# Rotary embedding on one core: loads issued eight tiles ahead, alternating with the stores in one software queue

## The chip, the cores and the metric

The kernel runs on one core of a Trainium2 chip. The time is that of the device for one execution, in microseconds (us); the median over several executions is compared. The kernel uses three parts of the core: VectorE (DVE in the profile) computes, GpSimd (POOL) issues every DMA, and the core's 16 DMA engines move the data between the chip's memory (HBM) and the on-chip SBUF.

## The reference

`x` has 8 batches, 2048 positions, 8 heads and 64 values per head, in float32: 33.55 MB. The output has the same shape and type. `cos` and `sin` have 2048 positions by 32 values.

```
x1, x2 = x[..., :32], x[..., 32:]
out1 = x1 * cos - x2 * sin
out2 = x1 * sin + x2 * cos
out  = concatenate([out1, out2], axis=-1)
```

Each input value is read once and each output value is written once; only the two small tables are used again.

## The kernel before

**Tiles.** The 2048 positions are laid over 128 partitions, 16 neighbouring positions to each. A tile is one batch and four of these 16 positions: 128 partitions by 4 x 512 = 2048 values. There are 8 x 4 = 32 tiles. In HBM a tile is 1 MB of float32, in 128 contiguous pieces of 8 KB; in SBUF it is 512 KB of bfloat16. The conversion in either direction is made by the DMA itself, so that a load reads 1 MB and writes 512 KB, and a store reads 512 KB and writes 1 MB.

**Loads and stores.** All DMAs are issued by POOL (`nc.gpsimd.dma_start`) and so go through one software queue, in the order in which the program writes them: first the two tables (L44, L45), then all 32 loads (L70) from a loop of their own, then the 32 stores (L101) from the loop that computes. POOL runs its instructions in this order. Before it issues one, it waits for what that DMA needs, and everything behind it waits too. The tile framework gives the DMAs of this queue eight completion semaphores in turn, so that a DMA also waits until the one eight places before it has landed: never more than eight are under way.

**Compute.** For each tile DVE runs four instructions: `t1 = x * cos` (L91) and `t2 = x * sin` (L92) over the whole tile, then a subtraction (L98) and an addition (L99) over half a tile each, which put the output tile `ot` together. The framework's scheduler orders them over neighbouring tiles: through much of the program L91 of the next tile stands before L98 of this one.

**Buffers.** 20 for the input tiles (`xpool`), 4 each for `t1` and `t2`, 12 for the output tiles (`opool`). Load 20 and later ones wait until DVE is done with the tile 20 places before. L98 of tile 12 and later ones waits until the store of the tile 12 places before has landed; as the first store stands behind the last load in the queue, DVE can run no further than 12 output tiles before that.

Of the kernel before, what the change touches and what calls it, by code (L numbers as in the profile page):

```python
# [2 lines left out]

# [4 lines left out]


@with_exitstack  # L10
def kernel(
    ctx: ExitStack,
    tc: tile.TileContext,
    x: bass.AP,
    cos: bass.AP,
    sin: bass.AP,
    out: bass.AP,
):
    nc = tc.nc
    f32 = mybir.dt.float32  # L20
    bf16 = mybir.dt.bfloat16

    B, S, H, D = x.shape
    Dh = D // 2
    P = 128
    HD = H * D
    R = S // P

    SL = 4
    n_blk = R // SL  # L30
    FREE = SL * HD
    NH = SL * H
    NK = NH * 2

    xv = x.rearrange("b (q r) h d -> b q r (h d)", q=P)
    ov = out.rearrange("b (q r) h d -> b q r (h d)", q=P)

    cos_src = cos.rearrange("(q r) d -> q r d", q=P)
    sin_src = sin.rearrange("(q r) d -> q r d", q=P)

    const_pool = ctx.enter_context(tc.tile_pool(name="const", bufs=1))
    cos_sb = const_pool.tile([P, R, Dh], bf16, tag="cb")
    sin_sb = const_pool.tile([P, R, Dh], bf16, tag="sb")
    nc.gpsimd.dma_start(out=cos_sb, in_=cos_src)  # L44
    nc.gpsimd.dma_start(out=sin_sb, in_=sin_src)  # L45

    num_tiles = B * n_blk

    xpool = ctx.enter_context(tc.tile_pool(name="xpool", bufs=20))
    tpool = ctx.enter_context(tc.tile_pool(name="tpool", bufs=4))  # L50
    opool = ctx.enter_context(tc.tile_pool(name="opool", bufs=12))

    def coef(tab, l):
        a = tab[:, l * SL, :]
        return dataclasses.replace(
            a, ap=[a.ap[0][:], [Dh, SL], [0, 2 * H], a.ap[1][:]]
        )

    def idx(t):
        b = t // n_blk  # L60
        l = t % n_blk
        return b, l

    eng = nc.vector

    xts = []
    for t in range(num_tiles):
        b, l = idx(t)
        xt = xpool.tile([P, FREE], bf16, tag="xt", name=f"xt{t}")
        nc.gpsimd.dma_start(  # L70
            out=xt.rearrange("p (r f) -> p r f", r=SL),
            in_=xv[b, :, l * SL : (l + 1) * SL, :],
        )
        xts.append(xt)

    for t in range(num_tiles):
        b, l = idx(t)
        xt = xts[t]

        t1 = tpool.tile([P, FREE], bf16, tag="t1")  # L80
        t2 = tpool.tile([P, FREE], bf16, tag="t2")
        ot = opool.tile([P, FREE], bf16, tag="ot")

        cb = coef(cos_sb, l)
        sb = coef(sin_sb, l)

        xtv = xt.rearrange("p (r k d) -> p r k d", r=SL, d=Dh)
        t1k = t1.rearrange("p (r k d) -> p r k d", r=SL, d=Dh)
        t2k = t2.rearrange("p (r k d) -> p r k d", r=SL, d=Dh)

        eng.tensor_mul(out=t1k, in0=xtv, in1=cb)  # L91
        eng.tensor_mul(out=t2k, in0=xtv, in1=sb)  # L92

        t1v = t1.rearrange("p (h d) -> p h d", d=D)
        t2v = t2.rearrange("p (h d) -> p h d", d=D)
        otv = ot.rearrange("p (h d) -> p h d", d=D)

        eng.tensor_sub(out=otv[:, :, 0:Dh], in0=t1v[:, :, 0:Dh], in1=t2v[:, :, Dh:D])  # L98
        eng.tensor_add(out=otv[:, :, Dh:D], in0=t2v[:, :, 0:Dh], in1=t1v[:, :, Dh:D])  # L99

        nc.gpsimd.dma_start(  # L101
            out=ov[b, :, l * SL : (l + 1) * SL, :],
            in_=ot.rearrange("p (r f) -> p r f", r=SL),
        )


# [1 line left out]
_INS = ['x', 'cos', 'sin']  # L108
_OUTS = [((8, 2048, 8, 64), 'float32')]


# [23 lines left out]
```

## Time and profile before

| | us |
|---|---|
| median of 5 runs | 169.62 |
| lowest and highest of the 5 | 168.74, 170.59 |
| the profiled execution's own time | 170.7 |
| its span (first to last instruction) | 168.9 |
| DVE busy, 128 instructions | 111.7 |
| POOL busy, 70 instructions | 35.3 |

The span is the part of the profiled execution that the trace covers; 1.8 us of its time lie around it. The page gives the busy time of each engine, then the span in 40 equal slices of 4.2 us with the busy share of the engines and the DMA engines and the data rate, then the DMA queue, the chain of work that ended last, and the groups of instructions with their waits. The rate in GB/s counts the bytes that a DMA writes at its destination: for a load that is bfloat16, half of what it reads. A DMA share above 1 means that the records of neighbouring packets on a DMA engine overlap a little. A POOL line with an idle time and "<-DMA xt" says that POOL waited until a load had landed.

### The profile page before, as it was taken

How to read it: one execution, taken by the hardware profiler on the slowest of the kernel's cores; microseconds unless marked ns; L12 is line 12 of the kernel's file. 1: busy time of each engine (PE TensorE's matmuls, PEld its weight loads, DVE VectorE, ACT ScalarE, POOL GpSimd, SP SyncE). 2: the span in 40 equal slices, each digit the busy share in tenths (PEclk: the TensorE clock that was granted, in tenths of full speed). 3: DMA queues.
4: the chain of work that ended last, by engine and by line, in shares of the span. 5: the costliest groups of instructions: out<-in, count | busy, mean ns of one | idle time of the engine just before them, and what ended most of it. 6: DMA issues, size and time to landing. Idle time of an engine off the chain costs nothing.

```text
span 168.9 us, 282 instructions
## 1 busy us (share of the span) xinstructions
DVE 111.7 (66%) x128; POOL 35.3 (21%) x70
## 2 busy tenths in 40 slices
DVE  0049999999999960000007999999999999960000
POOL 7512122212212221221122122122212112120000
DMA  4999999999999999999999999999999999999940
GB/s 54 175 207 216 210 212 214 216 210 212 216 214 210 213 215 213 211 213 214 254 416 423 431 431 431 423 425 433 429 427 425 429 431 427 429 427 427 431 188 2
DMA packets 9506, 50.61 MB, mean 300 GB/s; under 512 B 1056, under 2 KB 1312, under 8 KB 5408
## 3 DMA queue, kind: packets, MB, share of 16 engines
q0 software_dynamic: 9504, 50.60, 103.2%
q14 instruction: 2, 0.02, 0.0%
HBM read 34.08 MB, written 33.55 MB: 400 GB/s over the span
## 4 chain that ended last, share of the span: by engine, by line
DMA 51%; DVE 24%; issue 12%; POOL 2%; POOLq 0%; DVEq 0%; PEldq 0%
DMA xt<-in_x_dram 39%; DMA out_dram<-ot 12%; DVE t L91 8%; DVE t L92 6%; DVE ot L98 5%; DVE ot L99 5%; POOL out_dram L101 2%; POOL cos_sb L44 0%; POOLq L130 0%; POOL sin_sb L45 0%; POOLq L101 0%; DVEq L98 0%; PEldq L130 0%; POOLq L70 0%
## 5 line engine op out<-in xcount | busy, mean ns | idle before, releaser
L91 DVE TENSOR_TENSOR t<-xt,cos_sb 128x2048 bf16<-128x2048 bf16 x32 | 38.9, 1216 | 11.1 <-DMA xt<-in_x_dram 10.9
L98 DVE TENSOR_TENSOR ot<-t,t 128x1024 bf16<-128x1024 bf16 x32 | 21.8, 681 | 27.7 <-DMA out_dram<-ot 27.7
L92 DVE TENSOR_TENSOR t<-xt,sin_sb 128x2048 bf16<-128x2048 bf16 x32 | 38.9, 1215 | 0.0
L101 POOL DMA_DIRECT2D out_dram<-ot x32 | 17.0, 532 | 65.9 <-DMA out_dram<-ot 29.1
L70 POOL DMA_DIRECT2D xt<-in_x_dram x32 | 16.9, 541 | 49.1 <-DMA xt<-in_x_dram 47.2
L99 DVE TENSOR_TENSOR ot<-t,t 128x1024 bf16<-128x1024 bf16 x32 | 21.8, 682 | 0.0
L44 POOL DMA_DIRECT2D cos_sb<-in_cos_dram x1 | 0.7, 667 | 0.8 <-PEq L130 0.8
L45 POOL DMA_DIRECT2D sin_sb<-in_sin_dram x1 | 0.5, 540 | 0.0
L119 POOL MEMSET const-float32-0.0<- 128x1 f32 x1 | 0.1, 98 | 0.2 <-issue 0.2
L119 POOL MEMSET const-bfloat16-1.0<- 128x1 bf16 x1 | 0.1, 101 | 0.0
L119 POOL MEMSET const-float32-1.0<- 128x1 f32 x1 | 0.1, 98 | 0.0
L119 POOL MEMSET const-uint8-127<- 128x1 uint8 x1 | 0.1, 98 | 0.0
## 6 DMA issues: line engine op xcount, KB each, us to landing
out_dram<-ot POOLq DMA_DIRECT2D x32, 1024.0 KB, 19.1
xt<-in_x_dram POOLq DMA_DIRECT2D x32, 512.0 KB, 19.1
cos_sb<-in_cos_dram POOLq DMA_DIRECT2D x1, 128.0 KB, 3.0
sin_sb<-in_sin_dram POOLq DMA_DIRECT2D x1, 128.0 KB, 3.0
```

The costliest lines, as they stand in the source:

```text
L44: nc.gpsimd.dma_start(out=cos_sb, in_=cos_src)
L45: nc.gpsimd.dma_start(out=sin_sb, in_=sin_src)
L70: nc.gpsimd.dma_start(out=xt.rearrange("p (r f) -> p r f", r=SL), in_=xv[b, :, l * SL : (l + 1) * SL, :],)
L91: eng.tensor_mul(out=t1k, in0=xtv, in1=cb)
L92: eng.tensor_mul(out=t2k, in0=xtv, in1=sb)
L98: eng.tensor_sub(out=otv[:, :, 0:Dh], in0=t1v[:, :, 0:Dh], in1=t2v[:, :, Dh:D])
L99: eng.tensor_add(out=otv[:, :, Dh:D], in0=t2v[:, :, 0:Dh], in1=t1v[:, :, Dh:D])
L101: nc.gpsimd.dma_start(out=ov[b, :, l * SL : (l + 1) * SL, :], in_=ot.rearrange("p (r f) -> p r f", r=SL),)
L119: nc = _bacc.Bacc("TRN2", target_bir_lowering=False, num_devices=1)
```

## The change

The loads leave their own loop. Eight loads are issued ahead of the computing loop; then each turn t of that loop first issues load t + 8 and at its end, as before, store t. In POOL's program the order becomes: the tables, loads 0 to 8, store 0, load 9, store 1, load 10, and so on to store 22, load 31, and then stores 23 to 31. The number of DMAs, their shapes, the buffers and DVE's instructions are unchanged. In DVE's program the scheduler's order of the 128 instructions shifts a little: through the first 18 tiles L91 of the next tile stands before L98 of this one, and from tile 19 on the four instructions of a tile stand together. All lines after the edit stand seven lower: loads L72, stores L108, DVE L98, L99, L105, L106.

```diff
-    xts = []
-    for t in range(num_tiles):
+    AHEAD = 8
+    xts = {}
+
+    def load(t):
         b, l = idx(t)
         xt = xpool.tile([P, FREE], bf16, tag="xt", name=f"xt{t}")
         nc.gpsimd.dma_start(
             out=xt.rearrange("p (r f) -> p r f", r=SL),
             in_=xv[b, :, l * SL : (l + 1) * SL, :],
         )
-        xts.append(xt)
+        xts[t] = xt
+
+    for t in range(AHEAD):
+        load(t)
 
     for t in range(num_tiles):
         b, l = idx(t)
         xt = xts[t]
+        if t + AHEAD < num_tiles:
+            load(t + AHEAD)
```

## The prediction

> **What bounds the kernel now.** I read the page's rows of slices first, then stretches of the span with DMA share and rate, then the waits, then the timeline of POOL, and the chain last.
>
> ```profile
> DMA  4999999999999999999999999999999999999940
> GB/s 54 175 207 216 210 212 214 216 210 212 216 214 210 213 215 213 211 213 214 254 416 423 431 431 431 423 425 433 429 427 425 429 431 427 429 427 427 431 188 2
> ...
> HBM read 34.08 MB, written 33.55 MB: 400 GB/s over the span
> ```
>
> The DMA engines are full from the second slice to the 38th. The rate has two plateaus because it counts bytes at the destination: 213 in the loads, which is 426 read from HBM, and 427 in the stores. Per HBM byte both stages run alike, one after the other.
>
> ```profile
> core 0: us, DVE busy (x) POOL busy (x), PEclk, DMA share, GB/s
> ...
> 10.00:82.00 72.00, 50.96 (x56) 15.33 (x29) 1.00 1.06 213
> ...
> 88.00:150.00 62.00, 60.25 (x72) 12.08 (x23) 1.00 1.12 428
> 150.00:160.00 10.00, 0.52 (x1) 0.67 (x2) 1.00 1.12 426
> ```
>
> From 150 to 160 us DVE and POOL are done and the rate is unchanged: the queue still drains. So DVE never set the rate, although it is busy for 60 of the 62 us before.
>
> ```profile
> POOL xt L70 <- DMA xt<-in_x_dram: 47.2, 23, 4.4
> POOL out_dram L101 <- DMA out_dram<-ot: 29.1, 15, 2.3
> DVE ot L98 <- DMA out_dram<-ot: 27.7, 1, 27.7
> POOL out_dram L101 <- DVE ot L99: 21.7, 9, 2.9
> ```
>
> POOL mostly waits for a DMA eight places earlier to land. DVE's 27.7 us are its wait for a free output buffer. The nine waits on DVE come last in the program; they shorten the queue but, by the stretches above, don't empty it.
>
> ```profile
> 2.44 4.24 POOL L70 DMA_DIRECT2D xt<-in_x_dram  x8
> 10.94 1.23 DVE L91 TENSOR_TENSOR t<-xt,cos_sb 128x2048 bf16<-128x2048 bf16 x1 [10.94 <-DMA xt<-in_x_dram]
> 11.12 0.53 POOL L70 DMA_DIRECT2D xt<-in_x_dram  x1 [4.44 <-DMA xt<-in_x_dram]
> ...
> 87.30 0.53 POOL L101 DMA_DIRECT2D out_dram<-ot  x1 [1.88 <-DMA xt<-in_x_dram]
> ...
> 89.84 0.53 POOL L101 DMA_DIRECT2D out_dram<-ot  x1 [2.00 <-DMA out_dram<-ot]
> ...
> 146.13 0.53 POOL L101 DMA_DIRECT2D out_dram<-ot  x1 [2.94 <-DVE ot L99]
> ...
> 149.61 0.53 POOL L101 DMA_DIRECT2D out_dram<-ot  x1 [2.94 <-DVE ot L99]
> 150.81 0.53 POOL L101 DMA_DIRECT2D out_dram<-ot  x1 [0.67 <-DVE ot L99]
> ```
>
> The view of the output tensor adds how long its stores took from issue to landing:
>
> ```profile
> DMA to landing us min/median/max: 13.4/19.1/19.5
> ```
>
> An issue stands 0.28 us behind the landing that it waited for. Load 0 lands at 10.84 (first L91 at 10.94), load 31 at 87.30 - 0.28 = 87.02: (87.30 - 11.12)/31 = 2.457 us per load. The shortest landing, 13.4 us, fits store 30: 149.61 + 13.4 = 163.0, and store 31 one step later, at about 165.5. So a store takes (165.5 - 87.0)/32 = 2.45 us. DVE at its own pace needs 149.61 - 146.13 = 3.48 us per tile.
>
> **The sum of the span now:** 10.84 (first load down) + 31 x 2.457 + 32 x 2.45 + 3.4 (end of the program, 168.9 - 165.5) = 168.8 of 168.9.
>
> ```profile
> DMA 51%; DVE 24%; issue 12%; POOL 2%; POOLq 0%; DVEq 0%; PEldq 0%
> ```
>
> The chain has 24% on DVE. That is no gain to be had: it follows a store back to the DVE tile that released its issue, but that store then stood 13 us or more in a full queue.
>
> **The change, part by part.**
>
> *The same 66 DMAs.* None is removed, added or resized; POOL's 64 issues of about 0.54 us (35 us) stay. What moves is order: stores 0 to 22 go ahead of loads 9 to 31. Each load moved past k stores lands 2.45k later, each store as much earlier. Nothing of the sum changes unless a DMA engine runs empty or a DMA's 2.45 us change.
>
> *The added wait at the start.* POOL now holds load 9 behind store 0, and store 0 needs tile 0 computed. DVE starts at 10.94 and needs L91, L92, L91 of the next tile (in by 13.3), L98 and L99: end 15.7 as in the timeline before. Store 0 goes at 15.9, load 9 at 16.5 instead of 13.57. At 15.9 loads 0 to 2 have landed (10.84 + 2 x 2.457 = 15.75), so loads 3 to 8, six DMAs or 14.7 us of work, cover the 2.9 us. Cost 0; without cover it would be 2.9 us, once.
>
> *The wait in the steady state.* Behind each waiting store stand all later loads. A pair of load and store takes 4.91 us in the queue, a tile on DVE 3.48. Store t is ready at 15.7 + 3.48t. Its place in the queue (the DMA eight before it landed) opens at 23.4 for store 2 (ready 22.7), 28.3 for store 3 (26.2), 33.2 for store 4 (29.7): the margin grows, and the queue holds eight again from load 10 on. Cost 0; the cover is gone only if DVE needed over 4.91 us per tile, and then each tile would pay the excess.
>
> *Buffers.* Load t + 8 overwrites tile t - 12, L98 of tile t needs store t - 12, landed long before. DVE's 27.7 us wait disappears and turns into waits of about 4.91 - 3.48 = 1.4 us per tile for its load. Both lie beside a full queue: worth 0.
>
> *The end.* Load 31 is followed by stores 23 to 31. It lands at 10.84 + 8 x 2.457 + 23 x 4.91 = 143.4; DVE finishes its tile 3.5 us later, store 31 goes at about 147.2 (150.81 now). Stores 24 to 30, seven, are then under way, so it lands in its turn, nine stores after load 31: 165.5. Cost 0.
>
> *The switches of direction.* This is the one price that the trace hardly shows. Before, the queue switches once from loads to stores and never back. After, 24 times to stores and 23 times back: 46 more. The one switch: from 87.30 to 89.84 is 2.54 where 2.457 is usual, +0.08 us.
>
> ```profile
> 83.00:83.50 0.50, 0.00 (x0) 0.00 (x0) 1.00 1.02 213
> 83.50:84.00 0.50, 0.00 (x0) 0.00 (x0) 1.00 1.05 328
> 84.00:84.50 0.50, 0.00 (x0) 0.00 (x0) 1.00 1.23 442
> ```
>
> In these half microseconds, while the engines go over to stores, the share stays above 1 and the rate climbs without a dip: no engine stops. The 0.08 us then look like a later landing of stores, which a switch back returns. Bounds per switch: above, for the unseen way back, a transfer that finds the pipe empty, `cos_sb`, with 3.0 us from issue to landing less 0.6 us for its 128 KB at 213 GB/s, so 2.4 x 23 = 55 us, far off; below nothing, the next load's reads overlapping the store's writes. A load writes and a store reads half of what passes the wide side, so with both ways wholly apart a pair would take 12/16 of its time: -1.23 us x 23 = -28 us. I take 0, the value nearest to the share at the switch.
>
> Weighed here: the rows say 426 read and 427 written, each alone. The Trainium skill, "DMA: Bandwidth & Descriptors", section "Latency and other measured facts", gives copies from HBM to HBM 214 GB/s in each direction as the full rate, 428 together; by it a mix has no more than one direction alone, the 67.6 MB take 158 us either way, and the sum stays. It speaks against a gain. The same page, "Two DMAs through the same engine are not ordered", says that the read and write sides of an engine are separate queues and descriptors are pipelined, which allows the overlap; by it the sum could fall by up to the 28 us. No run here mixes the two yet.
>
> **Sum:** span 168.9 + 0 = 168.9. The profiled execution took 170.7, 1.1 above the median; with no change in the span the forecast is the median, 169.6 us.
>
> **Rivals.**
>
> *Each switch costs (slower).* Place: the DMA engines, at each of 46 switches. At the row's 0.083 us: 46 x 0.083 = 3.8, so 173.4. It decides from 1.7/46 = 0.037 us on, which is 1% of the time. At twice the row it is 177. For it: the one switch did come late, and the way back is unseen. Against: the share without a dip.
>
> *Reads run ahead of writes (faster).* If at each way back an engine has read one packet of the next load while the store's last writes go out: a load is 8 packets on each engine (128 pieces over 16), so 2.457/8 = 0.31 us x 23 = 7.1, so 162.5. At the whole overlap, 169.6 - 28 = 141, with 3.68 us per pair just above DVE's 3.48. For it: shares of 1.06 and 1.12 say that neighbouring packets overlap already, by a few hundredths. Against: load and store take the same 2.45 us, as if the wide side alone counted, whichever it is.
>
> *The queue runs dry behind a store that waits for DVE (slower).* Needs a tile over 4.91 us; each 0.1 us above that is 2.3 us over 23 pairs. Against: DVE keeps 3.48, and even its four mean durations laid end to end (1216, 1215, 681 and 682 ns) are 3.79. Under 3 in 100, held within the slower share.
>
> **How the numbers follow.** About 1%, 1.7 us, is what a measurement here can tell from no change. No change in the DMA's rate: 0.50, its own range 168 to 171.3. Switches cost, or the queue runs dry: 0.30, of which 0.10 above 177. Reads run ahead: 0.20, of which 0.07 below 157, twice the one packet and a little less. The range 157 to 177 leaves out 0.17. Faster 0.20, same 0.50, slower 0.30.
>
> **What would show it.** Right: the two plateaus become one of about 320 GB/s in the slices between 30 and 145 us (a load's 0.524 and a store's 1.049 MB written in 4.91 us), the DMA share stays above 1, POOL's waits alternate between loads and stores landing, DVE waits 1.4 us per tile, the last store is issued near 147 us. Dear switches: a plateau under 315, pairs of POOL issues over 5 us apart. Overlap: a plateau over 325. A dry queue: tenths under 9 in the DMA row and long POOL waits on L106. I am wrong if the pair differs from 4.91 us by over 0.07.

## The result: 0.4% slower, and the profile after

| | before | after |
|---|---|---|
| median, us | 170.06 (93 runs) | 170.77 (53 runs) |
| lowest and highest, us | 168.44, 171.10 | 169.48, 171.44 |
| span of the profiled execution, us | 168.9 | 169.2 |

The ratio after to before is 1.0041, 95% interval 1.0030 to 1.0052. That is inside the 1% that the prediction called no change, and 1.2 us from its 169.6. But with this many runs the interval leaves out 1: the change costs 0.71 us, where the prediction's sum says 0.

The two plateaus have become one, as foreseen. From the page of after, the DMA share and the rate in 40 slices:

```profile
DMA  4999999999999999999999999999999999999960
GB/s 53 169 200 212 216 214 266 305 307 322 334 333 325 319 308 310 311 332 334 331 323 301 311 313 331 334 329 323 307 312 309 326 330 360 432 430 422 422 248 2
```

Stretches of after (columns as before):

```profile
core 0: us, DVE busy (x) POOL busy (x), PEclk, DMA share, GB/s
...
10.00:28.00 18.00, 17.24 (x19) 3.73 (x7) 1.00 1.06 210
...
34.00:142.00 108.00, 87.02 (x99) 23.48 (x45) 1.00 1.09 320
...
148.00:160.00 12.00, 0.00 (x0) 0.13 (x1) 1.00 1.12 428
```

The mixed stage runs at 320 GB/s with a share of 1.09, between 1.06 of the loads and 1.12 of the stores. POOL's waits changed places:

```profile
POOL out_dram L108 <- DMA out_dram<-ot: 49.3, 22, 2.6
POOL xt L72 <- DMA xt<-in_x_dram: 38.0, 23, 4.2
DVE t L98 <- DMA xt<-in_x_dram: 32.4, 19, 10.7
POOL out_dram L108 <- DMA xt<-in_x_dram: 12.3, 6, 2.7
POOL out_dram L108 <- DVE ot L106: 12.0, 4, 4.4
```

DVE's single wait of 27.7 us for an output buffer is gone. In its place stand waits for a load: 19, of which the first, 10.7 us, is the one at the start that before has too, and the other 18 make 21.7 us; POOL waits for DVE four times only. POOL's timeline in after:

```profile
15.84 0.54 POOL L108 DMA_DIRECT2D out_dram<-ot  x1 [4.42 <-DVE ot L106]
16.37 0.54 POOL L72 DMA_DIRECT2D xt<-in_x_dram  x1
...
31.01 0.53 POOL L72 DMA_DIRECT2D xt<-in_x_dram  x1 [1.66 <-DMA xt<-in_x_dram]
...
124.25 0.53 POOL L72 DMA_DIRECT2D xt<-in_x_dram  x1 [1.58 <-DMA xt<-in_x_dram]
...
147.60 0.53 POOL L108 DMA_DIRECT2D out_dram<-ot  x1 [2.95 <-DVE ot L106]
```

Store 0 and load 9 go at 15.84 and 16.37 (foreseen 15.9 and 16.5), the last store at 147.60 (147.2). From load 12 at 31.01 to load 31 at 124.25 lie 19 pairs: 4.907 us each, against 2.457 + 2.45 = 4.907 before. The chain names DVE no more:

```profile
DMA 81%; issue 3%; POOL 3%; POOLq 0%; PEldq 0%
```

Where, then, are the 0.71 us? The stretches of one microsecond around the first store, of before and of after:

```profile
25.00:26.00 1.00, 1.00 (x2) 0.10 (x1) 1.00 1.00 201
26.00:27.00 1.00, 1.00 (x2) 0.43 (x1) 1.00 1.14 229
27.00:28.00 1.00, 1.00 (x2) 0.00 (x0) 1.00 1.07 213
```

```profile
25.00:26.00 1.00, 1.00 (x3) 0.37 (x1) 1.00 1.21 229
26.00:27.00 1.00, 1.00 (x1) 0.16 (x1) 1.00 1.04 152
27.00:28.00 1.00, 1.00 (x2) 0.00 (x0) 1.00 0.94 209
```

In after the rate falls to 152 GB/s between 26 and 27 us, while the share of that microsecond is 1.04: the engines are not idle, their packets take longer. By the trace's packet records a packet of a load takes 0.324 us in the even stream; between 24 and 28 us 37 of them take over 0.4 in after, the longest 0.91, and none in before. The first packet of a store begins at 27.51, so the slow ones run ahead of it. They belong, but for those of the engines that lag, to load 8, the last load ahead of the first store. The trace also keeps, for each DMA, the moment at which each of the 16 engines reported its part. I call the mean of these 16, less that of the DMA before, the step of a DMA. It is 2.455 us on average in the even stream of both kernels; that of load 8 is 2.93 in after, 0.47 late, and 2.456 in before. Nothing later in after stands out so. The start differs as well, ahead of anything that the change moves: load 1 lands, on the mean, at 10.63 in before and 10.92 in after, and over the other profiles with this start (g2 aside) between 10.2 and 11.7. The slowest engine, which ends the program, runs behind the mean by 2.6 us at the end of before and by 2.1 at the end of after, so this one pair of spans (168.94 and 169.16 before rounding) shows only 0.2 of the difference.

### The profile page after: what moved, and what is told of

Read it like the earlier page. It is cut to its first block, busy times and chain, and to the rows that moved or that the text cites. A ratio compares the mean times of both kernels' runs of the same rounds, so it can differ in the third digit from the quotient of the medians.

```text
span 169.2 us, 292 instructions
## 1 busy us (share of the span) xinstructions
DVE 114.3 (68%) x128; POOL 35.4 (21%) x70
## 4 chain that ended last, share of the span: by engine, by line
DMA 81%; issue 3%; POOL 3%; POOLq 0%; PEldq 0%
DMA out_dram<-ot 68%; DMA xt<-in_x_dram 13%; POOL xt L72 2%; POOL cos_sb L44 0%; POOLq L137 0%; POOL sin_sb L45 0%; POOLq L108 0%; PEldq L137 0%
## 5 line engine op out<-in xcount | busy, mean ns | idle before, releaser
L98 DVE TENSOR_TENSOR t<-xt,cos_sb 128x2048 bf16<-128x2048 bf16 x32 | 39.1, 1221 | 32.5 <-DMA xt<-in_x_dram 32.4
L99 DVE TENSOR_TENSOR t<-xt,sin_sb 128x2048 bf16<-128x2048 bf16 x32 | 38.9, 1217 | 0.0
L108 POOL DMA_DIRECT2D out_dram<-ot x32 | 17.1, 535 | 73.7 <-DMA out_dram<-ot 49.3
L72 POOL DMA_DIRECT2D xt<-in_x_dram x32 | 16.9, 542 | 38.0 <-DMA xt<-in_x_dram 38.0
L105 DVE TENSOR_TENSOR ot<-t,t 128x1024 bf16<-128x1024 bf16 x32 | 22.0, 686 | 0.5
L106 DVE TENSOR_TENSOR ot<-t,t 128x1024 bf16<-128x1024 bf16 x32 | 21.8, 682 | 0.0
```

Source lines behind the costliest of these rows:

```text
L72: nc.gpsimd.dma_start(out=xt.rearrange("p (r f) -> p r f", r=SL), in_=xv[b, :, l * SL : (l + 1) * SL, :],)
L108: nc.gpsimd.dma_start(out=ov[b, :, l * SL : (l + 1) * SL, :], in_=ot.rearrange("p (r f) -> p r f", r=SL),)
```

## The experiments

Theory A: one stall at the first turn from loads to stores. Its rivals: B, each of the 46 added turns costs 0.015 us; C, the late load is chance. All times are medians; a ratio is to the kernel before, run on the same chip, with its 95% interval. "Late" is the step of the last load ahead of the first large store, less 2.455 us.

### The change again, one early store, groups of four, twenty ahead

The changed kernel unchanged (e1):

> The changed kernel once more, for a second profile. In its first profile the load/store pairs keep 4.91 us, but load 8, the last one ahead of the first store, lands 0.47 us late on the mean of the 16 engines. Theory A, one stall at the first turn from loads to stores: load 8 is late again by 0.3 to 0.6 us and no other DMA is by over 0.15. Theory B, each of the 46 added turns costs a little (0.7/46 = 0.015 us): no single late DMA is needed, and DMAs 12 to 56 take over 2.455 us each. Theory C, the late load was chance: it is gone or elsewhere, and the time is still about 0.4% up. All three expect a ratio near 1.004.

One early store (e2), in place of the load in the loop:

```diff
+        if t == 0:
+            load(AHEAD)
+        if t == 1:
+            for u in range(AHEAD + 1, num_tiles):
+                load(u)
         xt = xts[t]
-        if t + AHEAD < num_tiles:
-            load(t + AHEAD)
```

> Loads 0 to 8, store 0, then loads 9 to 31 and stores 1 to 31: one store among the loads, two added turns instead of 46. Theory A: load 8 late by 0.3 to 0.6 us as in the changed kernel, ratio about 1.003 to 1.004. Theory B: 2 x 0.015 us, ratio 1.000. Theory C: ratio 1.000 if it takes the long mixed stage, no late load at a fixed place.

Groups of four (e3):

```diff
-        if t + AHEAD < num_tiles:
-            load(t + AHEAD)
+        if t % 4 == 0:
+            for u in range(t + AHEAD, min(t + AHEAD + 4, num_tiles)):
+                load(u)
```

> Loads 0 to 11 ahead, then four stores and four loads in turn: 10 added turns instead of 46. Theory A: load 11, the last ahead of the first store, late by 0.3 to 0.6 us, ratio about 1.003 to 1.004. Theory B: 10 x 0.015 = 0.15 us, ratio 1.001. Theory C: no late DMA at a fixed place.

Twenty ahead (e4), `AHEAD = 20`:

> Twenty loads ahead instead of eight, all that the input buffers hold: 11 pairs alternate instead of 23, 22 added turns. Theory A: the late load moves to load 20, the last ahead of the first store, 0.3 to 0.6 us, ratio about 1.003 to 1.004. Theory B: 22 x 0.015 = 0.33 us, ratio 1.002. Theory C: no late DMA at a fixed place.

| | added turns | late | us | ratio |
|---|---|---|---|---|
| e1 | 46 | load 8: 0.41 | 170.77 | 1.0045 (1.0006 to 1.0084) |
| e2 | 2 | load 8: 0.77 | 170.74 | 1.0044 (1.0016 to 1.0071) |
| e3 | 10 | load 11: 0.23 | 170.63 | 1.0062 (1.0032 to 1.0092) |
| e4 | 22 | load 20: 0.00 | 170.15 | 1.0025 (0.9991 to 1.0059) |

The late load comes back, and it moves with the first store: C falls as far as the place goes. Two added turns cost as much as 46, so B, by which e2 would stand at 1.000, can't be the whole of it. But the size varies from 0 to 0.77, and the interval of e4 allows no statement on a time without the stall.

### How early the first turn is, and whether a small store can take it first

`AHEAD = 4`, `12` and `16` (f1, f2, f3):

> Four loads ahead instead of eight: the first store stands behind load 4. In the profiles so far the last load ahead of the first store is late by 0.47, 0.41 and 0.77 us on the mean of the engines (load 8, three profiles), by 0.23 (load 11), by 0.0 (load 20). Theory A1, the earlier the first turn the dearer: load 4 late by 0.4 us or more, ratio 1.004 or more. Theory A2, it is there or not by chance: anything from 0 to 0.8.

> Twelve loads ahead: the first store stands behind load 12. Theory A1: load 12 late by 0.1 to 0.3 us. Theory A2: anything from 0 to 0.8.

> Sixteen loads ahead: the first store stands behind load 16. Theory A1: load 16 late by 0 to 0.15 us. Theory A2: anything from 0 to 0.8.

A small early store (f4), in the loop of the first eight loads:

```diff
+    z = const_pool.tile([P, 128], bf16, tag="z")
+    nc.vector.memset(z, 0.0)
+    spare = nc.dram_tensor("spare_dram", (P, 128), f32, kind="Internal").ap()
     for t in range(AHEAD):
         load(t)
+        if t == 1:
+            nc.gpsimd.dma_start(out=spare, in_=z)
```

> The changed kernel with one more store, of 32 KB of zeros in SBUF to a spare 64 KB in HBM, between load 1 and load 2; it adds about 0.2 us of transfer. Theory A3, the first store of a program pays once wherever it stands: load 8 is on time (under 0.15 us late), and the price lies at loads 1 and 2, beside their disorder at the start. Theory A1, the turn itself while the stream is young costs: load 8 is late by 0.4 to 0.8 us as in the changed kernel.

With four ahead the first store stands behind load 5 and not, as expected, behind load 4: in POOL's timeline of f1 six loads go first. Load 5 is 0.80 late (f1: 170.66 us, 1.0065, 1.0028 to 1.0102), load 12 0.33 (f2), load 16 0.00 (f3). In f4 load 8 is on time (170.61 us, 1.0033, 1.0000 to 1.0066). This looked like "the earlier the dearer" and like a first store that pays for all. The next runs put both to the test.

### Sixteen ahead timed, a late start, a tiny store, the tables moved

> Sixteen loads ahead, now timed: no late load in its first profile, but 30 added turns are left. Theory A, the stall at the first turn is the whole difference: ratio 1.000, within 0.001. Theory B, each turn costs 0.7/46 us: 30 x 0.015 = 0.46 us, ratio 1.0027.

The late start (g2):

```diff
+    idle = const_pool.tile([P, 2048], bf16, tag="idle")
+    nc.vector.memset(idle, 0.0)
+    for _ in range(28):
+        nc.vector.tensor_mul(out=idle, in0=idle, in1=idle)
+    nc.vector.tensor_copy(out=cos_sb[:, 0, 0:1], in_=idle[:, 0:1])
+    nc.vector.tensor_copy(out=sin_sb[:, 0, 0:1], in_=idle[:, 0:1])
...
+        if t <= AHEAD:
+            nc.vector.tensor_copy(out=xt[:, 0:1], in_=idle[:, 0:1])
```

> The changed kernel with about 32 us of work on VectorE that nothing uses in front of the first DMA (28 more multiplications of 1.14 us, and one small copy into each table and each of the first nine input tiles, which makes their loads wait). Eight ahead as in the changed kernel, so the first store comes as early in the stream, but at about 58 us after the start of the program instead of 27. Theory A1a, what counts is how young the stream of DMAs is: load 8 is late by 0.4 us or more. Theory A1b, what counts is the time since the program began (no late load was seen with first stores at 47 us and after): load 8 is under 0.15 us late. The span grows by about 32 us in either case.

The tiny store (g3) is f4 with `[P, 16]` in place of `[P, 128]`:

> The changed kernel with one tiny early store between loads 1 and 2, 4 KB of zeros in SBUF to a spare 8 KB in HBM. Theory A3: the first store of the program has been made, load 8 is on time, and the time is that of before: ratio 1.000 to 1.001. If the turn needs a larger store to count, or if the stall is not what the time shows: load 8 late, or ratio 1.004.

The tables behind two loads (g4), on the kernel before:

```diff
-    nc.gpsimd.dma_start(out=cos_sb, in_=cos_src)
-    nc.gpsimd.dma_start(out=sin_sb, in_=sin_src)
...
         xts.append(xt)
+        if t == 1:
+            nc.gpsimd.dma_start(out=cos_sb, in_=cos_src)
+            nc.gpsimd.dma_start(out=sin_sb, in_=sin_src)
```

> The kernel before with the two tables loaded behind loads 0 and 1 instead of ahead of them. In all profiles the first two loads take packets of up to 1.5 us on some of the engines, and the slowest engine stays 1 to 3 us behind to the end. Theory S1, the tables' small packets bring that disorder about: the first two loads run regularly, the slowest engine's lag shrinks under 0.8 us, ratio 0.985 to 0.995. Theory S2, it comes with any start of all 16 engines: same lag, ratio 1.000.

- g1: 170.24 us, 1.0049 (1.0018 to 1.0080), and load 16 is 0.25 late in this profile. f3 is the same kernel and had 0.00. With the irregular start one profile doesn't settle the size of a stall.
- g2: span 205.2, first store at 64.5 us, load 8 late by 0.65. The time since the program began is not what counts.
- g3: 170.98 us, 1.0072 (1.0038 to 1.0107), load 8 late by 0.65. A tiny store ahead doesn't help.
- g4: 167.87 us (167.81 to 168.02 in 6 runs), 0.9897 (0.9867 to 0.9928). Faster than both kernels, and its times spread over 0.2 us, where those of before, beside it, spread from 168.28 to 170.85.

The tail shows what g4's start changes. Stretches of before, and of the same g4 kernel in its second run (h2 below):

```profile
160.00:162.00 2.00, 0.00 (x0) 0.00 (x0) 1.00 1.12 426
162.00:164.00 2.00, 0.00 (x0) 0.00 (x0) 1.00 0.21 74
164.00:166.00 2.00, 0.00 (x0) 0.00 (x0) 1.00 0.03 12
```

```profile
160.00:162.00 2.00, 0.00 (x0) 0.00 (x0) 1.00 0.95 356
162.00:164.00 2.00, 0.00 (x0) 0.00 (x0) 1.00 0.01 4
```

Before ends with a share of 0.03 from 164 us on: less than one of 16 engines at work, while the others are done. I take it for the engine that fell behind in the first loads and never caught up: the trace doesn't name the engine of a report, but in every load and store of before the last of the 16 comes 2.6 to 2.8 us behind the mean. With the tables behind two loads no engine falls far behind (0.57 and 0.56 us at the end in the two profiles, 2.57 in before).

### The same orders on the regular start

This start lets the orders be told apart to 0.1 us. All four were run on one chip; the diffs are those above put together.

> The changed kernel with the tables loaded behind loads 0 and 1, which made the start regular in the kernel before (lag of the slowest engine 0.57 us instead of 2.57, ratio 0.990). Theory A, the late load at the first turn is a rest of the disorder at the start: no load late by over 0.15 us, time as the kernel before with the same tables, ratio 0.990 within 0.001. Theory A1, a turn in a young stream costs in any case: load 8 late by 0.4 to 0.7 us, ratio 0.992 to 0.995. Theory B, each added turn costs 0.015 us: no late load, DMAs 12 to 56 over 2.46 us each, ratio 0.994.

> The kernel before with the tables behind loads 0 and 1, once more, on the same chip as the three others of this call: the base that they are held against. All theories: ratio 0.990, lag under 0.8 us.

> Tables behind loads 0 and 1, four loads ahead: the first store stands behind load 4, at about 20 us. Theory A: no late load, ratio 0.990 within 0.001. Theory A1: load 4 late by 0.6 us or more, ratio 0.994 or more. Theory B: 54 added turns of 0.015 us, 0.8 us, ratio 0.995.

> Tables behind loads 0 and 1, loads 0 to 8, store 0, loads 9 to 31, stores 1 to 31: two added turns. Theory A: no late load, ratio 0.990 within 0.001. Theory A1: load 8 late by 0.4 to 0.7 us, ratio 0.992 to 0.995. Theory B: ratio 0.990.

| | added turns | late | us (lowest to highest) | ratio |
|---|---|---|---|---|
| h2, order of before | 0 | load 31: 0.00 | 167.95 (167.80 to 167.99) | 0.9871 (0.9843 to 0.9898) |
| h4, one early store | 2 | load 8: 0.52 | 168.29 (168.25 to 168.38) | 0.9893 (0.9866 to 0.9921) |
| h1, the change | 46 | load 8: 0.61 | 168.44 (168.36 to 168.50) | 0.9901 (0.9876 to 0.9926) |
| h3, four ahead | 52 | load 5: 0.71 | 168.50 (168.43 to 168.58) | 0.9905 (0.9880 to 0.9930) |

(Store 0's own step is 0.05 to 0.06 us long in all four, wherever it stands, and isn't counted here.) The late load is there on a regular start too: it is no rest of the disorder. The change costs 168.44 - 167.95 = 0.49 us here, and one early store alone 0.34; both ranges lie clear of that of h2, while those of h4 and h1 touch. The expected ratios went by 0.990 for h2, which came to 0.9871; so the four are held against each other. Over the last 53 steps, in h4 and h1 those behind load 9, the mean of the engines takes 130.12 us in h2, 130.12 in h4 and 130.10 in h1. So behind the first turn 44 more turns cost nothing on the mean of the engines, and B, which asks 0.66 us for them, falls. In the two profiles the 0.15 us between h4 and h1 lie in how far the slowest engine is behind the mean at the end, 0.36 against 0.50; whether the later turns bring that about is not shown.

The stall in stretches of one microsecond, h2, h4 and h1:

```profile
25.00:26.00 1.00, 1.00 (x2) 0.53 (x1) 1.00 1.07 217
26.00:27.00 1.00, 1.00 (x2) 0.00 (x0) 1.00 1.13 225
```

```profile
25.00:26.00 1.00, 1.00 (x2) 0.53 (x1) 1.00 1.29 217
26.00:27.00 1.00, 1.00 (x2) 0.00 (x0) 1.00 0.81 119
27.00:28.00 1.00, 1.00 (x3) 0.00 (x0) 1.00 1.08 377
```

```profile
25.00:26.00 1.00, 1.00 (x2) 0.54 (x1) 1.00 1.13 176
26.00:27.00 1.00, 1.00 (x2) 0.00 (x0) 1.00 0.94 131
27.00:28.00 1.00, 1.00 (x2) 0.00 (x0) 1.00 1.11 381
```

Over these first two microseconds h2 moves 442 KB, h4 336 and h1 307. At the loads' 213 GB/s the gaps are 0.50 and 0.63 us, the lateness of load 8 by another way. DVE is busy throughout in all three.

### The place of the first turn, and the small store, on the regular start

> Tables behind loads 0 and 1, sixteen loads ahead: the first store stands behind load 16. In the profiles with this start load 8 was late by 0.5 and 0.6 us and load 4 by 0.7, and the DMAs behind the first turn kept 2.455 us each whether they turn 44 times or once. Theory A1, the first turn costs more the younger the stream: load 16 late by 0 to 0.3 us, and the time follows it: 167.9 to 168.25 us, between the order of before (167.95) and one early store (168.29). If the first turn cost the same wherever it comes before the last load: load 16 late by 0.5 us, 168.4. If turns behind the first did cost: 168.3 or more with no late load.

> Tables behind loads 0 and 1, eight ahead as in the changed kernel, and one small store (32 KB of zeros in SBUF to a spare 64 KB in HBM, about 0.2 us of transfer) between loads 3 and 4. Theory A3 in the form that a store of this size ahead pays for the first turn: load 8 is under 0.15 us late, and whatever the first turn costs shows at load 3. Theory A1 without that: load 8 is late by 0.5 us as in the changed kernel with this start, time 168.6. In both, the DMAs behind the first large store keep 2.455 us each.

Both ran on another chip than the four above. i1: load 16 late by 0.37, 168.11 us (168.02 to 168.24), 0.9885 (0.9854 to 0.9916). On this start the first turn costs 0.71 at load 5, 0.5 to 0.6 at load 8, 0.37 at load 16 and nothing at load 31. i2: load 8 late by 0.49, 168.57 us (168.56 to 168.65), 0.9912 (0.9884 to 0.9940). Here the small store doesn't take the price of the first turn. Why load 8 was on time in f4 is not known; f3 and g1, one kernel with 0.00 and 0.25, show how far two profiles with the irregular start can differ.

## Why the prediction was right and where it was wrong

- **The bound, right.** The DMA engines were and are full; DVE's 27.7 us wait and POOL's new waits moved nothing. The chain's 24% on DVE disappeared without a gain.
- **The added wait at the start, the steady state, the buffers and the end, right.** Each issue time came within 0.6 us, the pair is 4.907 us, and no stretch shows an idle queue. DVE waits 1.2 to 1.3 us per tile for its load (foreseen 1.4).
- **"The switches of direction ... I take 0", wrong.** This is the step that failed. It priced 46 turns alike, by the one turn that before shows, behind 32 loads, and that turn is nearly free (load 31 is on time, store 0's step 0.06 us long). The price of the first turn depends on its place: behind nine loads it holds the load ahead of it up by 0.4 to 0.8 us in eight of nine profiles (f4 is the ninth). For the 44 turns that follow, 0 was right on the mean of the engines. On the regular start one early store alone makes 0.34 of the 0.49 us. The step went by the rate and the DMA share at that one turn. The share couldn't have shown the price anywhere: while load 8 is held up it is 1.04 at 152 GB/s, as the packets don't stop but take longer. Its reading of the 0.08 us, a later landing that the switch back returns, holds: in the mixed stage of after a store's step is about 2.50 us and a load's 2.41.
- **The rival "each switch costs", right in its sign, wrong in its mechanism.** At 46 x 0.083 it gave 173.4. It isn't a price per turn.
- **The rival "reads run ahead", wrong.** A pair takes the same time as a load and a store apart. On the two passages of the Trainium skill, "DMA: Bandwidth & Descriptors", weighed in the prediction: the measured copy rates (section "Latency and other measured facts"), by which a mix moves no more than one direction, agree with these runs, where each pair moves 2.1 MB of HBM traffic in 4.907 us, 427 GB/s. That the read and write sides of an engine are separate queues (section "Two DMAs through the same engine are not ordered") may be so, but no gain from it shows here.
- **The first term, 10.84 us to the first load, taken as given.** It held 1% that the change didn't touch: with the tables moved, the kernel before takes 0.9871 to 0.9897 of its time.

**What stays open.** Why packets of the load ahead of the first store take longer the earlier it comes. The time since the start of the program (g2), the disorder at the start (h1) and a store of 8 or 64 KB ahead of it (g3, i2) don't decide it. VectorE's work alone doesn't hold a load up: it is busy in h2 in the same microseconds, and in f3 at a first turn that cost nothing. But a part of it isn't excluded, and no run here tests it: wherever a load was held up at the first turn, VectorE was busy throughout, and at the first turns that are free behind 21 and 32 loads it was idle (busy 0.14 of 2.46 us in e4, 0 in before, g4 and h2). So the fall to nothing at load 31 may come from the idle VectorE as well as from the place; the fall from 0.71 to 0.37 does not, as VectorE was busy throughout in both. The trace doesn't show what an engine reads ahead. Open too is 0.2 us of the 0.71: the regular start shows 0.49, and whether the irregular one makes the stall larger or only the times more scattered was not settled. That the small packets of the tables cause the disorder at the start is argued; shown is that moving them ends it.

## What to carry to other kernels

Where the DMA engines are full from end to end, a new order of the same transfers is worth nothing by itself; look for what it costs at the places where the stream changes, and price a single turn by where it stands, not by the number of turns. A busy share says that engines don't stop, not that they move data at their rate: read it beside the rate. When the times of a kernel scatter by more than the effect, first find what scatters them: here a regular start cut the spread from 2.6 to 0.2 us, was worth more than the change under study, and made the rest measurable. A last slice with under one engine's share points to an engine that fell behind; here it did so at the start.

## What the hardware showed that was not expected

- The slowest of the 16 DMA engines was 2.8 us behind the mean at the first load (landing by the slowest engine at 10.84, by the mean at 8.07) and still 2.57 behind after 64 transfers. With the 256 KB of tables behind two loads it was 0.57.
- On the regular start the first turn of this software queue from loads to stores held the load ahead of it up by 0.71 us behind six loads, 0.5 to 0.6 behind nine, 0.37 behind seventeen and not at all behind 32 (VectorE idle there); later turns cost nothing on the mean of the engines, in either direction.
- Loads and stores mixed in one queue moved 427 GB/s of HBM traffic, as much as either alone.
